# Transposes and down products of an expert chunk placed one chunk behind its gate and up products, in a fixed order of three engines

## The chip, the cores and the metric

The kernel runs on one core of one Trainium2 chip. A core has five engines with queues of their own: TensorE (PE; its weight loads are shown as PEld), VectorE (DVE), ScalarE (ACT), GpSimd (POOL) and SyncE (SP), which here only issues DMA transfers. Sixteen DMA engines move data between HBM and the on-chip memory. The metric is the device time of one execution in microseconds; less is better.

## The reference, cut to what matters

One layer of a hybrid model over 512 tokens of width 1024: a convolution and a gated recurrence (the front part), then a mixture of 16 experts, then a norm. Each expert takes the 64 tokens with the highest affinity to it. The experts are what the change touches:

```python
aff = softmax(einsum('bnd,de->bne', v, router_w))
gate, idx = top_k(swapaxes(aff, 1, 2), 64)      # 64 of 512 tokens for each of 16 experts
xs = v[bidx, idx]
ys = (silu(xs @ wg) * (xs @ wu)) @ wd           # wg, wu: 1024 x 2816; wd: 2816 x 1024, per expert
out = zeros_like(v).at[bidx, idx].add(ys * gate[..., None])
```

All of it is float32. The weights of one expert are 3 x 2816 x 1024 values, 33 blocks of 1 MB (1.0486 million bytes); all 16 experts read 528 blocks once, and no block is used twice.

## The kernel before, in words

**The stream of loads.** The host lays out every weight block as one row of `in_stream`, 128 x 2048 values, in the order that `plan()` gives (L67 to L137). The kernel brings them in by one SP queue, in that order (`issue`, L199), into a ring of 22 buffers (8 + 7 + 7, L187), with two more blocks in another buffer at the start. `take(name, AHEAD)` (L220) issues all loads up to 23 blocks past the one that is asked for; a load into a buffer waits until the block that was there before has been used. For each expert and each chunk j the plan has the gate blocks, the up blocks and the down blocks of chunk j (L129 to L131); for the last two chunks of the last expert the up blocks of both come before the down blocks (L132 to L136).

**The chunks.** The 2816 hidden columns of an expert are cut into five chunks of 512 and one of 256 (`chunks`, L182). For a chunk TensorE multiplies the expert's tokens `xe` with the gate block (`pgu` bank 0) and the up block (bank 1), L1118: two blocks each, one each in the half chunk. ScalarE takes silu of the gate (L1126), VectorE multiplies with the up result (L1129), into `sg`. `turn` (L1036) transposes `sg` on TensorE (`ht`, L1042) and copies it on VectorE (`hT`, L1047). `products_down` (L1052) multiplies `hT` with the down blocks, summed over the chunks in `dn` (L1061).

**The order.** The loop at L1095 writes, for chunk j, first gate and up products of j, then `turn` and `products_down` of chunk j-1 (`pending`, L1133 to L1135). This is the order of the text; from L1121 on the framework's scheduler may reorder the instructions of each engine as they are built, apart from the last two chunks of the last expert, where the order of TensorE is written out (`manual_schedule`, L1103). A written order of all three engines holds over the end of the front part and ends with `tail.close()` at L1091, and again over the last steps from L1164. At run time each engine always works through its own instructions in the order in which they were built.

**Work between experts.** `scatter` (L1019) scales the result of the previous expert into `ys` (L1021), multiplies it with the one-hot rows `ohT` into `sc` (L1029) for four groups of 128 tokens, and adds to the sums `acc` (L1033). It stands behind the last down products of that expert. `combine_weights` (L995) makes `ohT` by transposes (`oht`, L999) at j = 2. `route` (L942) makes the next expert's ranks at j = 3: transposes `rk` on TensorE, comparisons `junk` on VectorE (L959 to L965), one-hot rows `ohr` on VectorE and GpSimd (L954). `gathered` (L971) collects the tokens of the next expert by products with `ohr` (`gx`, L978), two copies (`xg`, L982) and four transposes (`gt`, L985); `dispatch` (L989) makes `xe` in eight steps on VectorE (L992). The buffers for `sc`, `oht`, `rk` and `gt` are one pair of PSUM banks, tag "c".

**The end.** Behind the last down product stand the scaling of it (L1163), its scatter into four row groups (`fin`, L1082 and L1170), the final norm and four stores (L1208).

Of the kernel before, what the change touches and what calls it, by code (L numbers as in the profile page):

```python
# [17 lines left out]
P = 128  # L18
# [48 lines left out]
def plan():  # L67
# [57 lines left out]
    NJ = len(chunks)  # L125
    for e in range(NE):

        ends = e == NE - 1
        for j in range(NJ - 2 * ends):  # L129
            load_up(e, j)  # L130
            load_down(e, j)  # L131
        if ends:  # L132
            load_up(e, NJ - 2)
            load_up(e, NJ - 1)
            load_down(e, NJ - 2)
            load_down(e, NJ - 1)  # L136
# [4 lines left out]
def hybrid_layer(ctx: ExitStack, tc: tile.TileContext, x, vecs, wa, wi, router_w, stream, out):  # L141
# [798 lines left out]
    def route(e, then=None):  # L940
        pr = pc(f"rk{e}")[:, 0, :]
        for i in range(NT):  # L942
            T.transpose(pr[:, i * P:(i + 1) * P], aff[:, i, e:e + 1].to_broadcast([P, P]), ident)  # L943
        if then is not None:
            then()
        cnt = ex.tile([P, NT, 3], F32, tag="cnt", name=f"cnt{e}")
        V.memset(cnt, 0.0)
        junk = ex.tile([P, 512], F32, tag="ys", name=f"junk{e}", bufs=1)
        rank = ex.tile([P, NT], F32, tag="rank", name=f"rank{e}")
        ohr = ex.tile([P, NT, CAP], F32, tag="ohr", name=f"ohr{e}", bufs=1)  # L950

# [5 lines left out]
        for i in range(NT):  # L957
            v = aff[:, i, e:e + 1]
            V.tensor_scalar(junk[:, i * P:N], pr[:, i * P:N], v, None, op0=OP.is_gt, op1=OP.add,  # L959
                            accum_out=cnt[:, i, 0:1])  # L960
            if i:
                V.tensor_scalar(junk[:, 0:i * P], pr[:, 0:i * P], v, None, op0=OP.is_ge, op1=OP.add,
                                accum_out=cnt[:, i, 1:2])
            V.scalar_tensor_tensor(junk[:, i * P:(i + 1) * P], pr[:, i * P:(i + 1) * P], v, earlier,
                                   op0=OP.is_equal, op1=OP.mult, accum_out=cnt[:, i, 2:3])  # L965
            if i:
                ranked(i - 1)
        ranked(NT - 1)
        return ohr, rank

    def gathered(e, ohr):  # L971

        pg = p2(f"gx{e}")
        for i in range(NT):
            for q in range(2):
                for h in range(2):
                    c0 = h * 512 + q * 256
                    T.matmul(pg[64 * h:64 * h + 64, q, 0:256], ohr[:, i, :], x_sb[:, i, c0:c0 + 256],  # L978
                             start=i == 0, stop=i == NT - 1)
        xg = ex.tile([P, 512], F32, tag="ys", name=f"xg{e}", bufs=1)  # L980
        for q, cp in enumerate((V.tensor_copy, S.copy)):
            cp(xg[:, q * 256:(q + 1) * 256], pg[:, q, 0:256])  # L982
        px = pc(f"gt{e}")[:, 0, :]
# [3 lines left out]
        return [px[:, k // 4, k % 4, :] for k in range(KD)]  # L987

    def dispatch(e, px):  # L989
# [3 lines left out]
        return xe, last  # L993
# [25 lines left out]
    def scatter(e, ohT):  # L1019
        ys = ex.tile([P, 512], F32, tag="ys", name=f"ys{e}", bufs=1)  # L1020
        V.tensor_tensor(out=ys, in0=down.pop(e), in1=m5, op=OP.mult)  # L1021
        if e == 0:
# [3 lines left out]
        for i in range(NT):  # L1026
            sc = pc(f"sc{e}_{i}")
            for h in range(2):
                T.matmul(sc[:, h, :], ohT[64 * h:64 * h + 64, i * P:(i + 1) * P], ys[64 * h:64 * h + 64, :],  # L1029
                         start=True, stop=True)  # L1030
            for h in range(2):
                hs_ = slice(h * 512, (h + 1) * 512)
                V.scalar_tensor_tensor(acc3[:, i, hs_], sc[:, h, :], aff[:, i, e:e + 1], prev[:, i, hs_],  # L1033
                                       op0=OP.mult, op1=OP.add)

    def turn(st):  # L1036

        e, j, fw, h, _ = st
# [13 lines left out]
    def products_down(st, halves=(0, 1)):  # L1052
        e, j, fw, _, wdn = st
# [34 lines left out]

    ohr, rank = route(0, rest)
    xe, last_v = dispatch(0, gathered(0, ohr))  # L1090
    tail.close()  # L1091

    later = ExitStack()
    pending = None
    for e in range(NE):  # L1095
        ends = e == NE - 1
        if e:
            xe, _ = dispatch(e, gathered(e, ohr))
        for j, (f0, fw) in enumerate(chunks):
            hw = fw // 2  # L1100
            nl = fw // 256
            if ends and j == NJ - 2:
                later.enter_context(tc.manual_schedule(engines={mybir.EngineType.PE}))  # L1103
                below(0)
            if ends and j >= NJ - 2:
                turn(pending)
            if ends and j == NJ - 2:
                products_down(pending)
            pgu = p2(f"pgu{e}_{j}")
            for gu, nm in enumerate("gu"):  # L1110
                w = [take(f"{nm}{e}_{j}_{s}", AHEAD) for s in range(nl)]
                pp = pgu[:, gu, :]
                kl = KD // nl
                if ends and j == NJ - 1 and gu:
                    below(1, 0)
                for k in range(KD):
                    for h in range(2):
                        last_t = T.matmul(pp[64 * h:64 * h + 64, 0:hw], xe[:, k, :], w[k // kl][:, k % kl, h * hw:(h + 1) * hw],  # L1118
                                 start=k == 0, stop=k == KD - 1)
            if e == 0 and j == 0:  # L1120
                later.enter_context(tc.issue_after(last_t.ins))  # L1121
                later.enter_context(tc.issue_after(last_v.ins))
            pg, pu = pgu[:, 0, :], pgu[:, 1, :]
            wdn = [take(f"d{e}_{j}_{s}", AHEAD) for s in range(nl)]
# [6 lines left out]
            if ends and j == NJ - 1:  # L1131
                break
            if pending is not None and not (ends and j == NJ - 2):  # L1133
                turn(pending)
                products_down(pending)  # L1135
# [13 lines left out]
            if e == 0 and j == 3:  # L1149
                later.close()  # L1150
# [13 lines left out]
    later.enter_context(tc.manual_schedule(engines=ordered))  # L1164
# [57 lines left out]
    later.close()  # L1222
# [37 lines left out]
```

## Time and profile before

| | us |
|---|---|
| median of 3 runs | 1611.38 (1609.38 to 1611.47) |
| the profiled execution, its own time | 1612.04 |
| the profiled execution, span from its first to its last instruction | 1610.2 |
| TensorE busy in the span | 1415.2 (88%) |
| VectorE busy | 549.7 (34%) |
| ScalarE busy | 205.5 (13%) |
| moved by DMA | 601.06 MB, mean 373 GB/s |

The profile is of one execution. A busy share is an average over parts with different limits, and matmuls are pipelined, so a busy TensorE isn't one at its peak. The front part ends, and the first expert's products start, near 304 us; the rest of the span is the experts and some 15 us of ending. An idle stretch of an engine is put down to the instruction that released it. L12 is line 12 of the kernel before.

### The profile page before, as it was taken

How to read it: one execution, taken by the hardware profiler on the slowest of the kernel's cores; microseconds unless marked ns; L12 is line 12 of the kernel's file. 1: busy time of each engine (PE TensorE's matmuls, PEld its weight loads, DVE VectorE, ACT ScalarE, POOL GpSimd, SP SyncE). 2: the span in 40 equal slices, each digit the busy share in tenths (PEclk: the TensorE clock that was granted, in tenths of full speed). 3: DMA queues.
4: the chain of work that ended last, by engine and by line, in shares of the span. 5: the costliest groups of instructions: out<-in, count | busy, mean ns of one | idle time of the engine just before them, and what ended most of it. 6: DMA issues, size and time to landing. Idle time of an engine off the chain costs nothing.

```text
span 1610.2 us, 24198 instructions
## 1 busy us (share of the span) xinstructions
PE 1415.2 (88%) x10345; PEld 847.0 (53%) x10345; DVE 549.7 (34%) x1355; ACT 205.5 (13%) x360; POOL 145.7 (9%) x130
## 2 busy tenths in 40 slices
PE   6996869899988888888989898989898989898997
PEld 5764547676545445454545454545454545454553
DVE  4899995322240403031312121212222222222202
ACT  4676443200000000000000000000000000000001
POOL 3334555000000000000000000000000000000000
PEclk9998889999999999999999999999999999999999
DMA  9532547999999999999999999999999999999971
GB/s 380 188 131 82 206 192 331 363 412 407 422 426 424 425 424 426 424 423 425 425 425 425 424 425 424 425 425 425 425 423 426 424 425 424 425 425 425 424 301 53
DMA packets 86672, 601.06 MB, mean 373 GB/s; under 512 B 12397, under 2 KB 12709, under 8 KB 14117
## 3 DMA queue, kind: packets, MB, share of 16 engines
q1 hardware_dynamic: 86096, 599.10, 89.4%
q8 instruction: 81, 1.33, 0.3%
q10 hardware_dynamic: 469, 0.42, 0.1%
q14 instruction: 26, 0.21, 0.0%
HBM read 597.39 MB, written 2.10 MB: 372 GB/s over the span
## 4 chain that ended last, share of the span: by engine, by line
PE 79%; DVE 15%; issue 3%; ACT 3%; POOL 1%; DMA 0%; DVEq 0%; POOLq 0%; ACTq 0%
PE pgu L1118 39%; PE dn L1061 21%; PE sc L1029 4%; PE gx L978 4%; DVE y L538 3%; DVE sg L1129 1%; DVE hT L1047 1%; PE wocp L453 1%; PE ht L1042 1%; PE oht L999 1%; DVE junk L959 1%; ACT sg L1126 1%; PE pcv L474 1%; PE gt L985 1%; DVE u L593 1%
## 5 line engine op out<-in xcount | busy, mean ns | idle before, releaser
L1061 PE MATMUL dn<-d,hT 128*64 128x512 f32 x1384 | 369.6, 613 | 31.4 <-DVE hT L1047 31.4
L1118 PE MATMUL pgu<-g,xe 128*64 128x256 f32 (+1 forms) x3072 | 354.0, 362 | 0.4 <-DVE xe L992 0.4
L1118 PE MATMUL pgu<-u,xe 128*64 128x256 f32 (+1 forms) x3072 | 337.5, 363 | 0.0
L1118 PEld LDWEIGHTS pgu<-g,xe 128*64 128x64 f32 x3072 | 232.9, 137 | 133.8 <-issue 58.1
L1118 PEld LDWEIGHTS pgu<-u,xe 128*64 128x64 f32 x3072 | 222.3, 137 | 103.2 <-issue 22.9
L1129 DVE TENSOR_TENSOR sg<-sg,pgu 128x256 f32<-128x256 f32 x96 | 38.2, 398 | 594.0 <-ACT sg L1126 594.0
L1061 PEld LDWEIGHTS dn<-d,hT 128*64 128x64 f32 x1384 | 109.3, 139 | 194.6 <-issue 126.9
L1126 ACT ACTIVATE sg<-pgu 128x256 f32<-128x256 f32 x96 | 35.2, 366 | 1197.9 <-PE pgu L1118 1197.9
L954 POOL TENSOR_SCALAR ohr<-iota,rank,rinv 128x64 f32<-128x64 f32 x32 | 18.5, 578 | 1157.6 <-DVE rank L953 1157.6
L1033 DVE SCALAR_TENSOR_TENSOR acc<-sc,aff,acc 128x512 f32<-128x512 f32 x112 | 78.9, 747 | 65.6 <-PE sc L1029 65.6
L1042 PE MATMUL ht<-ident,sg 128*128 128x128 f32 x176 | 40.2, 303 | 57.0 <-DVE sg L1129 55.8
L1029 PE MATMUL sc<-ys,ohT 64*128 64x512 f32 x240 | 67.7, 641 | 16.5 <-DVE acc L1033 16.0
L538 DVE SCALAR_TENSOR_TENSOR y<-glu,dwt,y 128x480 f32<-128x480 f32 (+19 forms) x88 | 81.5, 973 | 0.2
L1042 PEld LDWEIGHTS ht<-ident,sg 128*128 128x128 f32 x176 | 18.3, 140 | 99.5 <-DVE sg L1129 90.3
L978 PE MATMUL gx<-x_sb,ohr 128*64 128x256 f32 x512 | 67.1, 380 | 0.4 <-POOL ohr L954 0.4
L1047 DVE COPY hT<-ht 128x256 f32<-128x256 f32 x95 | 38.0, 400 | 69.7 <-PE ht L1042 69.7
L1001 DVE TENSOR_SCALAR ohT<-oht 128x512 f32<-128x512 f32 (+1 forms) x16 | 11.1, 692 | 128.1 <-PE oht L999 128.1
L978 PEld LDWEIGHTS gx<-x_sb,ohr 128*64 128x64 f32 x512 | 46.6, 137 | 10.6 <-POOL ohr L954 1.1
L959 DVE TENSOR_SCALAR_CACHE_REDUCE junk<-rk,aff 128x512 f32<-128x512 f32 (+1 forms) x64 | 35.0, 546 | 37.2 <-PE rk L943 37.2
L992 DVE TENSOR_SCALAR xe<-gt,a,mods 128x64 f32<-128x64 f32 x128 | 33.8, 337 | 26.6 <-PE gt L985 26.6
L1029 PEld LDWEIGHTS sc<-ys,ohT 64*128 64x128 f32 x240 | 18.1, 184 | 37.5 <-DVE acc L1033 31.3
L577 PE MATMUL pg<-xc,gw 128*128 128x512 f32 x32 | 19.9, 708 | 17.6 <-ACT u L579 16.9
(319 smaller groups left out, 1190.7 us busy)
## 6 DMA issues: line engine op xcount, KB each, us to landing
g<-in_stream SPq DMA_DIRECT2D x176, 1024.0 KB, 19.6
u<-in_stream SPq DMA_DIRECT2D x176, 1024.0 KB, 19.6
d<-in_stream SPq DMA_DIRECT2D x173, 1024.0 KB, 19.6
adam<-in_stream SPq DMA_DIRECT2D x16, 1024.0 KB, 6.8
ada<-in_stream SPq DMA_DIRECT2D x8, 1024.0 KB, 10.9
cv<-in_stream SPq DMA_DIRECT2D x4, 1024.0 KB, 7.7
xs<-in_x SPq DMA_DIRECT2D x4, 512.0 KB, 8.1
lx<-in_stream SPq DMA_DIRECT2D x2, 1024.0 KB, 6.0
```

The source lines that it names most:

```text
L538: V.scalar_tensor_tensor(dst, src, tap(cb, t), dst, op0=OP.mult, op1=OP.add)
L959: V.tensor_scalar(junk[:, i * P:N], pr[:, i * P:N], v, None, op0=OP.is_gt, op1=OP.add, accum_out=cnt[:, i, 0:1])
L978: T.matmul(pg[64 * h:64 * h + 64, q, 0:256], ohr[:, i, :], x_sb[:, i, c0:c0 + 256], start=i == 0, stop=i == NT - 1)
L992: last = V.tensor_scalar(xe[:, k], px[k], a2[:, k:k + 1], SHIFT2[:, k:k + 1], op0=OP.mult, op1=OP.add)
L1029: T.matmul(sc[:, h, :], ohT[64 * h:64 * h + 64, i * P:(i + 1) * P], ys[64 * h:64 * h + 64, :], start=True, stop=True)
L1033: V.scalar_tensor_tensor(acc3[:, i, hs_], sc[:, h, :], aff[:, i, e:e + 1], prev[:, i, hs_], op0=OP.mult, op1=OP.add)
L1042: T.transpose(ptr[:, q2 * P:(q2 + 1) * P], h[:, q2 * P:(q2 + 1) * P], ident)
L1047: V.tensor_copy(hT[:, 0:nq, :], ptr[:, 0:nq * P].rearrange("p (q n) -> p q n", n=P))
L1061: T.matmul(down[e][64 * dh:64 * dh + 64, :], turned[j][:, q2, half * CAP:(half + 1) * CAP], wdn[qq // 2][:, qq % 2, dh * 512:(dh + 1) * 51 ...
L1118: last_t = T.matmul(pp[64 * h:64 * h + 64, 0:hw], xe[:, k, :], w[k // kl][:, k % kl, h * hw:(h + 1) * hw], start=k == 0, stop=k == KD - 1)
L1126: last_s = S.activation(sg[:, 0:hw], pg[:, 0:hw], AF.Silu)
L1129: V.tensor_tensor(out=sg[:, 0:hw], in0=sg[:, 0:hw], in1=pu[:, 0:hw], op=OP.mult)
```

## The change

The plan now gives, for every expert, the gate and up blocks of chunk j and then the down blocks of chunk j-1; the last down blocks of an expert come at its end. The written order of TensorE, VectorE and ScalarE holds from the end of the front part to the end of the kernel (`tail` is closed at the very end; `later` and its ties are gone). In it, chunk j is: gate products of j; silu; transposes and copy of j-1 (`turn`); extra work of this chunk, if any; up products of j; product of silu and up; down products of j-1, whose blocks are taken only there. The scatter of the previous expert is cut into four pieces, two each in chunks 0 and 1. The ranks are cut in two, tiles 0 and 1 in chunk 3, tiles 2 and 3 in chunk 4. At the end of an expert stand the gather of the next one, the transposes of the half chunk, the dispatch of the next expert, the down products of the half chunk, and the scaling into `ys`. The eight steps of `dispatch` go to VectorE and ScalarE by turns.

```diff
-    NJ = len(chunks)
     for e in range(NE):
-        ends = e == NE - 1
-        for j in range(NJ - 2 * ends):
+        for j in range(len(chunks)):
             load_up(e, j)
-            load_down(e, j)
-        if ends:
-            ...
+            if j:
+                load_down(e, j - 1)
+        load_down(e, len(chunks) - 1)
...
         xe = ex.tile([P, KD, CAP], F32, tag="xe", name=f"xe{e}", bufs=XEB)
         for k in range(KD):
-            last = V.tensor_scalar(xe[:, k], px[k], a2[:, k:k + 1], SHIFT2[:, k:k + 1], op0=OP.mult, op1=OP.add)
+            if k % 2:
+                S.activation(xe[:, k], px[k], AF.Identity, bias=SHIFT2[:, k:k + 1], scale=a2[:, k:k + 1])
+            else:
+                V.tensor_scalar(xe[:, k], px[k], a2[:, k:k + 1], SHIFT2[:, k:k + 1], op0=OP.mult, op1=OP.add)
...
     def products_down(st, halves=(0, 1)):
-        e, j, fw, _, wdn = st
+        e, j, fw, _ = st
+        wdn = [take(f"d{e}_{j}_{s}", AHEAD) for s in range(fw // 256)]
...
-    ohr, rank = route(0, rest)
-    xe, last_v = dispatch(0, gathered(0, ohr))
-    tail.close()
-    later = ExitStack()
-    pending = None
+    ohr, rank, ranks = route(0, rest)
+    ranks(0, 1, 2, 3)
+    xe = dispatch(0, gathered(0, ohr))
+    pending = ys = ohT = None
     for e in range(NE):
         ends = e == NE - 1
-        if e:
-            xe, _ = dispatch(e, gathered(e, ohr))
         for j, (f0, fw) in enumerate(chunks):
             ...
             pgu = p2(f"pgu{e}_{j}")
-            for gu, nm in enumerate("gu"):
-                ...
+            products_up(e, j, 0)
             sg = ex.tile([P, 256], F32, tag="sg", name=f"sg{e}_{j}")
-            last_s = S.activation(sg[:, 0:hw], pg[:, 0:hw], AF.Silu)
+            last_s = S.activation(sg[:, 0:hw], pgu[:, 0, 0:hw], AF.Silu)
             ...
-            V.tensor_tensor(out=sg[:, 0:hw], in0=sg[:, 0:hw], in1=pu[:, 0:hw], op=OP.mult)
-            st = (e, j, fw, sg, wdn)
-            if pending is not None and not (ends and j == NJ - 2):
-                turn(pending)
-                products_down(pending)
-                if pending[1] == NJ - 1:
-                    scatter(e - 1, ohT)
+            if j:
+                turn(pending)
+            if j < 2 and e:
+                scatter(e - 1, ohT, ys, 2 * j)
             if j == 2:
-                ohT, gate = combine_weights(e, ohr, rank)
-            pending = st
-            if j == 3 and e + 1 < NE:
-                ohr, rank = route(e + 1)
+                next_ohT, gate = combine_weights(e, ohr, rank)
+            if j == 3 and not ends:
+                ohr, rank, ranks = route(e + 1)
+                ranks(0, 1)
             ...
+            if j == 4 and not ends:
+                ranks(2, 3)
+            if ends and j == NJ - 2:
+                below(0)
+            if ends and j == NJ - 1:
+                below(1, 0)
+            products_up(e, j, 1)
+            V.tensor_tensor(out=sg[:, 0:hw], in0=sg[:, 0:hw], in1=pgu[:, 1, 0:hw], op=OP.mult)
+            st = (e, j, fw, sg)
+            if ends and j == NJ - 1:
+                break
+            if j:
+                products_down(pending)
+            if j < 2 and e:
+                scatter(e - 1, ohT, ys, 2 * j + 1)
+            if j == 2:
+                ohT = next_ohT
+            pending = st
+        if not ends:
+            xg = gathered(e + 1, ohr)
+            turn(st)
+            xe = dispatch(e + 1, xg)
+            products_down(st)
+            ys = weighted(e)
```

## Rows read from the trace of the kernel before

**Rows 1.** The page: busy time by engine; DMA share in 40 slices, in tenths

```profile
PE 1415.2 (88%) x10345; PEld 847.0 (53%) x10345; DVE 549.7 (34%) x1355; ACT 205.5 (13%) x360; POOL 145.7 (9%) x130
DMA  9532547999999999999999999999999999999971
```

**Rows 2.** Waits of TensorE, 400 to 1500 us: us in total, times, longest

```profile
PE ht L1042 <- DVE sg L1129: 52.8, 53, 1.2
PE dn L1061 <- DVE hT L1047: 30.4, 54, 0.7
PE sc L1029 <- DVE acc L1033: 14.9, 13, 1.1
PE rk L943 <- DVE ohT L1001: 10.6, 14, 0.8
PE gt L985 <- DVE xg L982: 3.4, 13, 0.3
```

**Rows 3.** Windows: stretch, length, busy by engine (count), TensorE clock, DMA share, GB/s

```profile
400.00:1500.00 1100.00, 986.80 (x7437) 550.08 (x7435) 257.31 (x815) 34.58 (x94) 16.18 (x28) 0.99 1.01 425
1570.00:1595.00 25.00, 23.56 (x178) 12.00 (x179) 1.89 (x6) 2.15 (x4) 0.00 (x0) 1.00 0.00 1
```

**Rows 4.** Waits of SP's queue, 400 to 1500 us, columns as in rows 2

```profile
SPq L217 <- DMA d<-in_stream: 308.1, 147, 3.3
...
SPq L217 <- PE dn L1061: 54.9, 45, 6.3
```

**Rows 5.** DMA queues, 400 to 1500 us: packets, MB, share of 16 engines

```profile
q1 hardware_dynamic: 63968, 465.87, 100.8%
```

**Rows 6.** Timeline of TensorE: start, length, line, operation, count, [idle before, releaser]

```profile
728.09 3.62 PE L1118 MATMUL pgu<-g,xe 128*64 128x256 f32 x32
...
736.11 0.44 PE L1042 MATMUL ht<-ident,sg 128*128 128x128 f32 x2 [0.94 <-DVE sg L1129]
737.07 3.65 PE L1061 MATMUL dn<-d,hT 128*64 128x512 f32 x16 [0.52 <-DVE hT L1047]
740.55 3.62 PE L1118 MATMUL pgu<-g,xe 128*64 128x256 f32 x32
...
773.36 0.44 PE L985 MATMUL gt<-ident,xg 128*128 128x128 f32 x2 [0.26 <-DVE xg L982]
```

**Rows 7.** One line's instructions (L985): ns min/median/max, first and last start

```profile
L985 PE MATMUL gt<-ident,xg x64: 272/300/332, 302.4 to 1512.2; 128*128 128x128 f32 x64
```

**Rows 8.** Timeline of the end, all engines, columns as in rows 6

```profile
1547.24 0.33 SPq L215 DMA_DIRECT2D d<-in_stream  x1
...
1593.03 1.89 PE L1061 MATMUL dn<-d,x_sb 128*64 128x512 f32 x8
...
1594.96 0.75 DVE L1163 SCALAR_TENSOR_TENSOR hTh<-dn,gate,m 128x512 fp32r<-128x512 f32 x1 [4.17 <-PE dn L1061]
```

**Rows 9.** DMA issues, 1546.6 to 1549 us: count, KB each, median us to landing

```profile
d<-in_stream SPq DMA_DIRECT2D x1, 512.0 KB, 17.1
```

**Rows 10.** Windows of 10 us, columns as in rows 3

```profile
320.00:330.00 10.00, 10.00 (x84) 7.71 (x82) 0.75 (x2) 0.39 (x1) 0.00 (x0) 1.00 0.96 371
390.00:400.00 10.00, 10.00 (x75) 7.70 (x74) 1.29 (x3) 0.38 (x1) 0.00 (x0) 1.00 0.97 364
470.00:480.00 10.00, 7.33 (x43) 3.58 (x41) 5.80 (x29) 0.38 (x1) 1.16 (x2) 0.86 1.02 428
590.00:600.00 10.00, 8.54 (x68) 4.61 (x66) 0.85 (x2) 0.39 (x1) 0.00 (x0) 1.00 1.01 417
800.00:810.00 10.00, 7.32 (x46) 3.29 (x46) 6.49 (x32) 0.38 (x1) 1.16 (x2) 1.00 1.01 425
```

**Rows 11.** The page's groups: count | busy us, mean ns | idle before, releaser

```profile
L1126 ACT ACTIVATE sg<-pgu 128x256 f32<-128x256 f32 x96 | 35.2, 366 | 1197.9 <-PE pgu L1118 1197.9
...
L959 DVE TENSOR_SCALAR_CACHE_REDUCE junk<-rk,aff 128x512 f32<-128x512 f32 (+1 forms) x64 | 35.0, 546 | 37.2 <-PE rk L943 37.2
L992 DVE TENSOR_SCALAR xe<-gt,a,mods 128x64 f32<-128x64 f32 x128 | 33.8, 337 | 26.6 <-PE gt L985 26.6
```

More of the change, by code (lines that the diff above doesn't have):

```diff
@@ L955, in ranked, with ranks @@
                             op0=OP.is_equal, op1=OP.mult)
[L957 to L969, printed above, removed]
+        def ranks(*tiles):
+            for i in tiles:
+                v = aff[:, i, e:e + 1]
+                V.tensor_scalar(junk[:, i * P:N], pr[:, i * P:N], v, None, op0=OP.is_gt, op1=OP.add,
+                                accum_out=cnt[:, i, 0:1])
+                if i:
+                    V.tensor_scalar(junk[:, 0:i * P], pr[:, 0:i * P], v, None, op0=OP.is_ge, op1=OP.add,
+                                    accum_out=cnt[:, i, 1:2])
+                V.scalar_tensor_tensor(junk[:, i * P:(i + 1) * P], pr[:, i * P:(i + 1) * P], v, earlier,
+                                       op0=OP.is_equal, op1=OP.mult, accum_out=cnt[:, i, 2:3])
+                if i:
+                    ranked(i - 1)
+            if i == NT - 1:
+                ranked(i)
+        return ohr, rank, ranks
     def gathered(e, ohr):
@@ L982, in gathered, with dispatch @@
             cp(xg[:, q * 256:(q + 1) * 256], pg[:, q, 0:256])
+        return xg
+    def dispatch(e, xg):
         px = pc(f"gt{e}")[:, 0, :]
@@ L986, in gathered @@
         px = px.rearrange("p (q h s) -> p h q s", h=2, s=CAP)
-        return [px[:, k // 4, k % 4, :] for k in range(KD)]
-    def dispatch(e, px):
+        px = [px[:, k // 4, k % 4, :] for k in range(KD)]
         xe = ex.tile([P, KD, CAP], F32, tag="xe", name=f"xe{e}", bufs=XEB)
         for k in range(KD):
-            last = V.tensor_scalar(xe[:, k], px[k], a2[:, k:k + 1], SHIFT2[:, k:k + 1], op0=OP.mult, op1=OP.add)
-        return xe, last
+            if k % 2:
+                S.activation(xe[:, k], px[k], AF.Identity, bias=SHIFT2[:, k:k + 1], scale=a2[:, k:k + 1])
+            else:
+                V.tensor_scalar(xe[:, k], px[k], a2[:, k:k + 1], SHIFT2[:, k:k + 1], op0=OP.mult, op1=OP.add)
+        return xe
     def combine_weights(e, ohr, rank):
@@ L1017, in hybrid_layer, with weighted, scatter @@
     down = {}
-    def scatter(e, ohT):
+    def weighted(e):
         ys = ex.tile([P, 512], F32, tag="ys", name=f"ys{e}", bufs=1)
         V.tensor_tensor(out=ys, in0=down.pop(e), in1=m5, op=OP.mult)
-        if e == 0:
+        return ys
+    def scatter(e, ohT, ys, i):
+        if not sums:
             sums.append(acc_tile("acc").rearrange("p (i d) -> p i d", i=NT))
@@ L1025, in scatter @@
         prev = x_sb if e == 0 else acc3
[L1026 to L1034, printed above, removed]
+        sc = pc(f"sc{e}_{i}")
+        for h in range(2):
+            T.matmul(sc[:, h, :], ohT[64 * h:64 * h + 64, i * P:(i + 1) * P], ys[64 * h:64 * h + 64, :],
+                     start=True, stop=True)
+        for h in range(2):
+            hs_ = slice(h * 512, (h + 1) * 512)
+            V.scalar_tensor_tensor(acc3[:, i, hs_], sc[:, h, :], aff[:, i, e:e + 1], prev[:, i, hs_],
+                                   op0=OP.mult, op1=OP.add)
     def turn(st):
-        e, j, fw, h, _ = st
+        e, j, fw, h = st
         nq = fw // 2 // P
@@ L1087, in rest, with products_up @@
         table(AF.Silu)
-    ohr, rank = route(0, rest)
-    xe, last_v = dispatch(0, gathered(0, ohr))
-    tail.close()
-    later = ExitStack()
-    pending = None
+    def products_up(e, j, gu):
+        f0, fw = chunks[j]
+        hw, nl = fw // 2, fw // 256
+        w = [take(f"{'gu'[gu]}{e}_{j}_{s}", AHEAD) for s in range(nl)]
+        kl = KD // nl
+        for k in range(KD):
+            for h in range(2):
+                T.matmul(pgu[64 * h:64 * h + 64, gu, 0:hw], xe[:, k, :], w[k // kl][:, k % kl, h * hw:(h + 1) * hw],
+                         start=k == 0, stop=k == KD - 1)
@@ L1163, in hybrid_layer @@
         V.scalar_tensor_tensor(dst, dn, gate, m5, op0=OP.mult, op1=OP.mult)
-    later.enter_context(tc.manual_schedule(engines=ordered))
     low(V, ysl, ys, ysh)
@@ L1221, in hybrid_layer @@
     rows_out(3, 1)
-    later.close()
+    tail.close()
 _OUT = (512, 1024)
```

29 lines of the change are left out of this document (removed).

## The prediction, made before the changed kernel was run

> **What bounds the kernel now.** I read the page's busy shares first. TensorE is busy 1415.2 us of 1610.2, and from the eighth of 40 slices on the 16 DMA engines are in the top tenth in nearly every slice [rows 1]. Two candidates for the bound, then, and an average can't choose between them. So the second view is the waits of TensorE over 400 to 1500 us, a stretch that holds nothing but experts: its idle time is ended by VectorE every time, never by a transfer in any amount [rows 2]. The windows view puts a size on it: 986.80 us busy of 1100, so 113.2 us idle, at DMA share 1.01 [rows 3]. The third view is the queue that issues the loads. SP mostly waits for an earlier load to land (d rows alone 308.1 us in 147 waits) and only 54.9 us in 45 waits for a down product to free a buffer [rows 4]. Loads are thus issued as fast as earlier ones land.
>
> So two streams run side by side at almost the same pace. The stream moves 465.87 MB in 1100 us [rows 5], 423.5 GB/s, so a 1.0486 MB load takes 2.476 us and an expert's 33 loads 81.7 us. TensorE needs from the gather of one expert to that of a later one (1512.2 - 773.4) / 9 = 82.1 us [rows 6, 7], of which 89.7% [rows 3], 73.6 us, are busy. TensorE never waits for a load because it runs behind the stream. How far behind shows at the end: the last load is issued at 1547.24 and takes 17.1 us, so it has landed at 1564.3 [rows 8, 9]; the down product that reads it starts at 1593.03 and ends at 1594.92 [rows 8]. From 1570 to 1595 the DMA engines carry next to nothing while TensorE is 94% busy [rows 3]. **That lag of 29 to 30 us after the last landing is what can be won, and the stream is the floor under it.**
>
> **The change part by part.** I go by the profiled execution: span 1610.2 us, its own time 1612.04, so 1.84 us lie around the span. The median of the three timed runs is 1611.38, 0.66 lower.
>
> *Transposes one chunk later.* A plain chunk now runs gate, up, wait 0.94, transposes 0.44, wait 0.52, down, and repeats after 740.55 - 728.09 = 12.46 us [rows 6]. The transposes wait for silu and product of the very chunk whose up products have just ended; the down products wait for the copy of the transposes. In the new order the transposes of chunk j-1 stand behind gate j (some 3.5 us of TensorE, after down j-2, itself 3.5 us behind the up products that they depend on), and the copy runs under up j (3.5 us). Both waits have a cover of over 3 us for under 1 us of work. Removed: 1.46 us a chunk, leaving 11.0 us, against 6 x 2.476 = 14.9 us of loads. In the stretch that is 52.8 + 30.4 us [rows 2].
>
> *Scatter in four pieces.* The four pairs of products now follow each other and wait up to 1.1 us for the sums of the one before (14.9 us) [rows 2]. Afterwards at least 3.4 us of gate, up or down products stand between two pieces. The sums go into VectorE's queue ahead of the product of silu and up; that product is needed only behind the next gate products. Removed: most of 14.9 us. The 10.6 us of the router's transposes behind the one-hot copy go the same way, since the two now stand in different chunks [rows 2].
>
> *Ranks in two halves.* Two tiles are some five passes of 0.55 us [rows 11], with the small steps 3 to 4 us by estimate, queued in VectorE ahead of the product of chunk 3 and of chunk 4. Those run under up products of 3.5 us; the result is wanted behind down (3.5) and gate (at least 1.8). Cost nothing. The GpSimd one-hots are wanted a chunk later still.
>
> *Gather and dispatch.* The gather now stands alone at the end of an expert, then one transpose pair of the last half chunk, then the four transposes, which wait for two copies. Nothing in the trace shows that exact order; the nearest row is the wait of 0.3 us there now [rows 2], with a copy of VectorE at some 0.5 us in a row with it (the wait of 0.52 behind the copy of the transposes [rows 6]), so 0 to 0.9 us an expert. I take 0.5. The eight xe steps are split over VectorE and ScalarE. ScalarE has no such step in the trace; its nearest row is 366 ns for the silu, VectorE's own step is 337 ns [rows 11], so four in a row take 1.3 to 1.5 us instead of 2.7 for eight. They hide behind the down products of the half chunk (8 matmuls, 1.89 us [rows 8]). Without that cover it is 1.5 us an expert. Either way it comes out of TensorE's spare time, not out of the end.
>
> *Loads in the order of use, down loads taken when used.* SP issues the same loads in another order. Now a down load sits in its buffer one chunk longer than its place in the ring, and every later load queues behind it in SP: the 54.9 us of SP waiting on down products [rows 4]. With several loads in flight most of this costs no bandwidth, since the share stays at 1.01. It cost some at the start: 371 GB/s in 320 to 330 and 364 in 390 to 400 [rows 10] against 424, together 1.25 + 1.4 = 2.7 us. I take that as won; the bounds are 0 and about 6 (twice that, if SP's waits in the steady part cost something too). What is lost before 310 stays, as those buffers only come free when expert 0 begins.
>
> **Sum.** TensorE would need 73.6 us an expert, perhaps 75 with new small waits, against 81.7 of the stream. It gains on the stream 6 to 8 us an expert, has the lag of 29 us used up within four or five experts, and waits for loads from then on. So **of 113 us of removed idle time only the lag counts**. The last landing moves from 1564.3 to 1561.6. Behind it half of the last eight down matmuls, 0.95 us (the last load comes in two halves), 0.1 for the start, and then the ending as it is, from 1594.92 to 1610.2, 15.3 us. Span 1561.6 + 1.05 + 15.3 = 1578.0; with 1.84 around it 1579.8; less the 0.66 by which the profiled execution stands above the median, **1579 us**, 2.0% faster.
>
> **Rivals.**
> *Part of the waits comes back.* Each engine works in its order, so in a new order other instructions can be held up by a late one than now. If 7 of the 8 us an expert return as other waits (the gather's copies, a queue behind the ranks), TensorE needs about 81 us and ends with about 15 us of lag left: 1594. Against it: each cover above is over 1 us longer than what it hides. Chance 0.07. If all comes back, nothing changes: 1611, chance 0.03; this is also the case in which the change doesn't do what it says.
>
> *The stream is not at its limit* and gains 1% when SP never waits for TensorE: 12 us off 1579, 1567. For it: SP waits 45 times for a down product in the steady part [rows 4]. Against it: the lowest 10 us window from 410 to 1550 still has 417 GB/s at share 1.01 [rows 10], though these waits come and go. Chance 0.05. The Trainium skill, "DMA: Bandwidth & Descriptors", section Specifications, states a fabric ceiling of 435 GB/s; by that an estimate of 2.41 us a load would end the stream some 30 us sooner, near 1548 in all. It also states 358 GB/s as a core's limit at the HBM, and there the trace disagrees with its 423.5.
>
> *TensorE waits for loads and its clock falls* (slower). In a plain chunk it would work 11.0 of 14.9 us, 74%. In the present trace two windows at 73% busy have a granted clock of 0.86 (some of the time at the level of 1.2 GHz) and 1.00 [rows 10], so such idling sometimes costs clock. Price: only 10.3% of the stretch is idle [rows 3], at a mean clock of 0.99, so below a mean clock of about 0.89 TensorE alone takes longer than now: from the transposes ahead of expert 0 at 302.4 [rows 7] to 1594.9 are 1292.5 us, 89.7% of them work, 1159; at 0.85 these become 1350, some 58 us more than now, 1669 in all. Against it: once TensorE is behind the stream it no longer waits for loads, and the clock over the experts as they are now is 0.99, so the fall would end itself. A mild form, with the ending alone at the lower clock, adds 2 to 4 us. The Trainium skill, "TensorE: Matmul & The Clock Gate", section "HAM oscillation", states that matmuls separated by waits for DMA can drop to half clock at each wait; the window at 1.00 shows that it need not happen at this busy share. Chance of slower 0.04.
>
> **How the numbers follow.** The forecast (stream as the floor) gets 0.81: 1574 with 6 us won at the loads, 1583 with none, 1587 with the mild clock loss. To leave out no more than 0.2 the range goes from 1571 to 1591; the rivals at 1567, 1594, 1611 and slower lie outside. Faster by over 0.2% (about what a measurement of this kernel can tell from no change): 0.93. Within 0.2%: 0.03. Slower: 0.04.
>
> **What would show it.** In the changed profile: TensorE's waits on the product of silu and up and on the copy are gone, and waits on loads stand in their place from about expert 5 on; the period of an expert there is 81.5 to 82 us, not 74; PE busy about 90% as before, since the floor sets the pace; GB/s in 320 to 400 without dips; the last load lands at 1558 to 1564 and the last down product ends 1 to 2 us after it. Wrong would be: the last down product over 5 us behind the last landing (order leaves waits), a period under 81 us (stream faster), or a granted clock under 0.95 over the experts.

## The result, and the profile after

| | before | after |
|---|---|---|
| median, us | 1611.43 (1609.38 to 1613.87, 4 runs) | 1583.43 (1582.49 to 1585.37, 4 runs) |
| ratio | | 0.9827 [0.981, 0.9844] |
| the profiled execution, its own time | 1612.04 | 1585.37 |
| its span | 1610.2 | 1583.5 |

28.0 us went, 1.7%; the prediction was 1579 with a range of 1571 to 1591. The same kernel measured again beside later experiments gave 1583.32 (0.9825 [0.9811, 0.9839]). The profiled execution of after is the slowest of its four, 1.94 us over their median.

The page of after: busy time by engine, DMA share in 40 slices, and the chain that ended last (followed back from the last instruction, at each step to what released it), by engine. Below it the chain of before.

```profile
PE 1412.9 (89%) x10345; PEld 797.5 (50%) x10345; DVE 542.8 (34%) x1291; ACT 231.4 (15%) x424; POOL 146.9 (9%) x130
DMA  9531547899999999999999999999999999999994
DMA 60%; PE 27%; DVE 10%; ACT 2%; issue 1%; POOL 0%; DVEq 0%; SPq 0%; ACTq 0%; POOLq 0%
```

```profile
PE 79%; DVE 15%; issue 3%; ACT 3%; POOL 1%; DMA 0%; DVEq 0%; POOLq 0%; ACTq 0%
```

Busy time of TensorE hardly moved against [rows 1], and neither did the DMA share. What moved is the chain: it now runs through loads for 60% of the span, where before it ran through TensorE for 79% and through loads for 0%. The busy shares would not have told.

Waits of TensorE in after, 400 to 1500 us (total, times, longest), to be read against [rows 2]:

```profile
PE pgu L1105 <- DMA g<-in_stream: 29.3, 55, 0.7
PE dn L1070 <- DMA d<-in_stream: 25.8, 48, 2.2
PE dn L1070 <- DVE sg L1145: 19.9, 34, 0.6
PE pgu L1105 <- DMA u<-in_stream: 12.2, 40, 0.5
PE gt L988 <- DVE xg L981: 3.8, 14, 0.3
```

The waits of the transposes, of the scatter and of the router's transposes are gone; loads stand in their place. The third row names VectorE's product, on which down products of the chunk before don't depend. A plain chunk shows what it is. Timeline of TensorE in after (start, length, line, operation, count, [idle before, releaser]):

```profile
1049.15 1.95 PE L1105 MATMUL pgu<-g,xe 128*64 128x256 f32 x16 [0.59 <-DMA g<-in_stream]
1051.49 1.95 PE L1105 MATMUL pgu<-g,xe 128*64 128x256 f32 x16 [0.39 <-DMA g<-in_stream]
1053.37 0.44 PE L1050 MATMUL ht<-ident,sg 128*128 128x128 f32 x2
1054.02 1.95 PE L1105 MATMUL pgu<-u,xe 128*64 128x256 f32 x16 [0.21 <-DMA u<-in_stream]
1056.35 1.95 PE L1105 MATMUL pgu<-u,xe 128*64 128x256 f32 x16 [0.38 <-DMA u<-in_stream]
1058.90 1.94 PE L1070 MATMUL dn<-d,hT 128*64 128x512 f32 x8 [0.60 <-DVE sg L1145]
1061.26 1.94 PE L1070 MATMUL dn<-d,hT 128*64 128x512 f32 x8 [0.42 <-DMA d<-in_stream]
1063.77 1.97 PE L1105 MATMUL pgu<-g,xe 128*64 128x128 f32 x32 [0.58 <-DMA g<-in_stream]
```

Six blocks, six starts, 2.44 us apart on average, (1063.77 - 1049.15) / 6: TensorE goes at the pace of the landings. The down products at 1058.90 keep that beat too, so their 0.60 us is read as a load as well, put down to an engine that ended a moment earlier (e4 below bears this out). With these rows 87 us of the 93 idle us (1100 - 1006.98, below) are waits for loads.

Windows of after, columns as in [rows 3]; then one window of before; then SP's waits for down products in 400 to 1500, as in [rows 4]:

```profile
300.00:400.00 100.00, 98.03 (x791) 55.45 (x789) 23.35 (x74) 9.12 (x22) 1.16 (x2) 1.00 0.98 404
310.00:320.00 10.00, 9.89 (x92) 6.29 (x88) 0.84 (x2) 0.38 (x1) 0.00 (x0) 1.00 1.01 388
320.00:330.00 10.00, 10.00 (x84) 5.58 (x82) 1.54 (x3) 0.38 (x1) 0.00 (x0) 1.00 1.02 424
390.00:400.00 10.00, 10.00 (x80) 4.95 (x76) 2.27 (x5) 0.38 (x1) 0.00 (x0) 1.00 1.01 428
540.00:550.00 10.00, 10.00 (x86) 5.75 (x86) 1.53 (x3) 0.38 (x1) 0.00 (x0) 1.00 1.02 420
1040.00:1050.00 10.00, 8.02 (x54) 3.47 (x52) 2.34 (x12) 0.00 (x0) 0.58 (x1) 1.00 1.01 424
400.00:1500.00 1100.00, 1006.98 (x7634) 525.10 (x7632) 256.52 (x776) 57.76 (x152) 16.17 (x28) 1.00 1.01 425
```

```profile
300.00:400.00 100.00, 98.35 (x776) 66.47 (x774) 22.80 (x75) 3.71 (x10) 1.16 (x2) 1.00 0.97 400
```

```profile
SPq L212 <- PE dn L1070: 2.1, 8, 0.3
```

TensorE still works without a pause at 540 to 550 and is down to 8.02 of 10 us at 1040 to 1050. SP's 54.9 us of waiting for down products are gone. The end of after, timeline of all engines, and the landing of its last load (count, KB, median us to landing), as in [rows 8, 9]:

```profile
1548.15 0.33 SPq L210 DMA_DIRECT2D d<-in_stream  x1
```

```profile
d<-in_stream SPq DMA_DIRECT2D x1, 512.0 KB, 17.1
```

```profile
1555.58 1.97 PE L1105 MATMUL pgu<-g,xe 128*64 128x128 f32 x32 [0.62 <-DMA g<-in_stream]
...
1566.42 1.89 PE L1070 MATMUL dn<-d,x_sb 128*64 128x512 f32 x8
...
1568.35 0.75 DVE L1175 SCALAR_TENSOR_TENSOR hTh<-dn,gate,m 128x512 fp32r<-128x512 f32 x1 [4.17 <-PE dn L1070]
```

The last load lands at 1548.15 + 17.1 = 1565.25, the last down product ends at 1568.31. **The last landing has hardly moved (1564.3 before); the lag behind it fell from 30.6 to 3.1 us.** That is 27.5 us. The two profiled spans differ by 26.7, since the last landing of after comes 0.9 us later and its ending is 0.1 us shorter; the medians differ by 28.0.

### The profile page after: what moved, and what is told of

It reads as the page before. It is cut to its first block, busy times and chain, and to the rows that moved or that the text cites. A ratio compares the mean times of both kernels' runs of the same rounds, so it can differ in the third digit from the quotient of the medians.

```text
span 1583.5 us, 24439 instructions
## 1 busy us (share of the span) xinstructions
PE 1412.9 (89%) x10345; PEld 797.5 (50%) x10345; DVE 542.8 (34%) x1291; ACT 231.4 (15%) x424; POOL 146.9 (9%) x130
## 4 chain that ended last, share of the span: by engine, by line
DMA 60%; PE 27%; DVE 10%; ACT 2%; issue 1%; POOL 0%; DVEq 0%; SPq 0%; ACTq 0%; POOLq 0%
DMA d<-in_stream 28%; DMA g<-in_stream 28%; PE pgu L1105 12%; PE dn L1070 5%; DVE y L533 4%; DMA u<-in_stream 4%; PE wocp L448 1%; PE gx L977 1%; PE sc L1037 1%; PE pcv L469 1%; DVE xc L562 1%; DVE u L588 1%; PE plx L448 1%; PE ht L1050 1%; PE pmada L337 0%
## 5 line engine op out<-in xcount | busy, mean ns | idle before, releaser
L1070 PE MATMUL dn<-d,hT 128*64 128x512 f32 x1400 | 331.9, 602 | 46.8 <-DMA d<-in_stream 26.1
L1105 PE MATMUL pgu<-g,xe 128*64 128x256 f32 (+1 forms) x3040 | 326.0, 364 | 31.0 <-DMA g<-in_stream 30.6
L1105 PE MATMUL pgu<-u,xe 128*64 128x256 f32 (+1 forms) x3072 | 331.5, 366 | 14.0 <-DMA u<-in_stream 12.2
L1105 PEld LDWEIGHTS pgu<-g,xe 128*64 128x64 f32 x3040 | 207.3, 137 | 183.9 <-PE dn L1070 48.3
L1105 PEld LDWEIGHTS pgu<-u,xe 128*64 128x64 f32 x3072 | 206.2, 137 | 135.5 <-ACT sg L1119 23.8
L1070 PEld LDWEIGHTS dn<-d,hT 128*64 128x64 f32 x1400 | 94.8, 137 | 229.9 <-issue 128.1
L1145 DVE TENSOR_TENSOR sg<-sg,pgu 128x256 f32<-128x256 f32 x96 | 38.3, 399 | 200.7 <-PE pgu L1105 200.7
L977 PE MATMUL gx<-x_sb,ohr 128*64 128x256 f32 x512 | 58.3, 379 | 0.0
L977 PEld LDWEIGHTS gx<-x_sb,ohr 128*64 128x64 f32 x512 | 37.7, 137 | 24.4 <-issue 8.9
L981 DVE COPY xg<-gx 128x256 f32<-128x256 f32 x16 | 6.8, 424 | 121.2 <-PE gx L977 121.2
L996 DVE TENSOR_SCALAR xe<-gt,a,mods 128x64 f32<-128x64 f32 x64 | 22.0, 344 | 36.5 <-ACT xe L994 23.6
```

The costliest lines, as they stand in the source:

```text
L1070: T.matmul(down[e][64 * dh:64 * dh + 64, :], turned[j][:, q2, half * CAP:(half + 1) * CAP], wdn[qq // 2][:, qq % 2, dh * 512:(dh + 1) * 51 ...
L1105: T.matmul(pgu[64 * h:64 * h + 64, gu, 0:hw], xe[:, k, :], w[k // kl][:, k % kl, h * hw:(h + 1) * hw], start=k == 0, stop=k == KD - 1)
L1145: V.tensor_tensor(out=sg[:, 0:hw], in0=sg[:, 0:hw], in1=pgu[:, 1, 0:hw], op=OP.mult)
```

## The experiments

Theory: the stream of loads is a floor with its end near 1565; TensorE's own pace counts only as far as it closes the lag behind the stream. Rivals: the gain goes with the waits removed; the load order carries it; the floor is something else. "Last landing" and "lag" below are read as above, from the last issue with its time to landing and the end of the last down products, in each one's profiled execution.

| kernel | median, us | ratio to before | last landing | lag |
|---|---|---|---|---|
| before | 1611.4 | | 1564.3 | 30.6 |
| after | 1583.4 | 0.9827 [0.981, 0.9844] | 1565.3 | 3.1 |
| after, measured again | 1583.3 | 0.9825 [0.9811, 0.9839] | 1563.2 | 3.0 |
| e1: old load order | 1589.0 | 0.9859 [0.9835, 0.9882] | 1565.7 | 6.4 |
| e2: shift undone | 1605.9 | 0.9966 [0.9954, 0.9977] | 1563.0 | 25.7 |
| e3: load order alone, engines as the scheduler places them | 1592.5 | 0.9884 [0.9866, 0.9901] | 1564.2 | 12.3 |
| e4: after, no down loads | 1453.8 | 0.9022 [0.8999, 0.9046] | | |
| e5: shift undone, no down loads | 1607.4 | 0.9968 [0.9956, 0.9979] | | |
| e6: 7.1 us more TensorE an expert | 1590.6 | 0.9864 [0.9846, 0.9882] | 1567.0 | 7.6 |
| e7: 14.2 us more | 1683.3 | 1.0443 [1.0419, 1.0468] | 1615.3 | 49.9 |
| e8: three buffers less | 1591.8 | 0.9875 [0.9859, 0.9891] | 1571.5 | 2.4 |
| e9: ending moved | 1581.8 | 0.9812 [0.9798, 0.9826] | 1562.6 | 1.2 |
| e10: old load order but in the last expert | 1584.3 | 0.9829 [0.9815, 0.9843] | 1565.3 | 4.3 |

**TensorE's own pace, without a third of the stream (e4, e5).** One down block is loaded once, and all down products read it; the other down loads are left out, and the ring has one buffer less for it.

```diff
-        wdn = [take(f"d{e}_{j}_{s}", AHEAD) for s in range(fw // 256)]
+        wdn = [dfix, dfix]
```

> The changed kernel without its 176 loads of down blocks: all down products read one block that is loaded once, so the result is another one; the ring has one buffer less to hold it. The stream falls to 22 loads an expert, 54.7 us at 2.488 us a load. Theory (the changed kernel waits for the stream, and TensorE alone would be faster): the expert takes TensorE's own time, 70.8 us as between experts 1 and 3 of the changed kernel, so 305 + 69 + 15 x 70.8 + 17 = 1453 us, 1440 to 1465, with hardly a wait of TensorE for a load. Rival (TensorE needs its 82 us an expert whatever the loads do): over 1560.

> The fixed order with the transposes and down products right behind the up products of the same chunk (the shift undone), and without the 176 loads of down blocks: all down products read one block, so the result is another one. It shows TensorE's own pace in that order. Theory: 80.4 us an expert, 1590 to 1610 us in all, and the same kernel with its loads is no faster than that and no faster than the stream lets it (1583). Rival (without the stream both orders are alike): as the changed kernel without these loads, about 1453.

The transposes of the gather show the pace: one line's instructions, ns min/median/max, first and last start. After, then e4, then e5:

```profile
L988 PE MATMUL gt<-ident,xg x64: 272/300/333, 304.1 to 1488.4; 128*128 128x128 f32 x64
```

```profile
L991 PE MATMUL gt<-ident,xg x64: 272/300/329, 301.3 to 1358.8; 128*128 128x128 f32 x64
```

```profile
L997 PE MATMUL gt<-ident,xg x64: 272/300/332, 303.3 to 1508.1; 128*128 128x128 f32 x64
```

Fifteen experts in each: 79.0, 70.5 and 80.3 us an expert. The new order needs 70.5 us when the stream lets it; in after it takes 79.0, and from the gather at 1077.00 to the one at 1487.78, five experts later, 82.2. A window of e4:

```profile
400.00:1400.00 1000.00, 993.03 (x7808) 542.33 (x7806) 263.88 (x794) 58.66 (x154) 16.28 (x28) 1.00 0.83 315
```

TensorE stands idle for 7 us of 1000 there, and the row "dn L1070 <- DVE sg L1145" of after (19.9 us) has no counterpart among its waits, although TensorE reaches the down products sooner: those 19.9 us were waits for down blocks.

Without the shift TensorE needs 80.3 us whether a third of the loads is there or not: 1607.4 without, 1605.9 with (next, where the same count also gives 80.3). So unshifted, TensorE is the bound; shifted, the stream is. Free of the stream the shift is worth 153.6 us; with it, 17 (e2 against e1, both in the old load order).

**The shift undone, the rest kept (e2).**

```diff
-            if j:
-                turn(pending)
+            if ends and j == NJ - 1:
+                turn(pending)
...
-            if j:
-                products_down(pending)
+            if not (ends and j == NJ - 2):
+                turn(st)
+                products_down(st)
```

> The changed kernel with the fixed order kept, but the transposes and down products of a chunk right behind its own up products, with the load order of before. Scatter in four pieces, split ranks and split dispatch stay. Theory (only the lag counts, and TensorE's own pace decides how much of it is closed): TensorE pays the two waits of 0.94 and 0.52 us again in each of six chunks and some 1 us at the gather, about 80.4 us an expert instead of 71, against 82.1 of the stream. It closes 1.7 us an expert, some 20 to 28 us of the 29 in all: 1585 to 1603 us. Rival (the shift is the whole gain): 1608 to 1612. Rival (the shift does nothing, the other parts carry the gain): 1582 to 1584, with no lag left behind the last landing.

Timeline of TensorE in e2, a plain chunk:

```profile
752.53 0.44 PE L1056 MATMUL ht<-ident,sg 128*128 128x128 f32 x2 [0.59 <-DVE sg L1151]
753.49 3.65 PE L1076 MATMUL dn<-d,hT 128*64 128x512 f32 x16 [0.52 <-DVE hT L1061]
```

1605.9, 3 us over the theory's range, and neither rival: both waits are back, the first shorter (0.59), and only 5.6 us of the gain are left. The pace was right (80.4 expected); the lag to be closed was not. It isn't the 29 us that before ended with, but what the stream is ahead after the first experts, and the first expert itself was slower here than in before's built order: TensorE worked 88.70 us of 300 to 400, against 98.35 in before (its row stands with the result). Window of e2:

```profile
300.00:400.00 100.00, 88.70 (x689) 46.79 (x687) 19.29 (x60) 6.93 (x18) 1.16 (x2) 1.00 0.98 403
```

**The old load order under the new engine order (e1), and in all but the last expert (e10).** In e1 `plan()` is that of before. In e10 experts 0 to 14 load the down blocks of chunk j behind the up blocks of j, and expert 15 loads as in after.

> The changed kernel with one part undone: the loads come in the order of before (down blocks of chunk j right behind its gate and up blocks), the order of the engines stays the new one. Theory (the stream of loads is the floor, and the engine order alone lets TensorE close the lag of 29 us): the stream carries the same bytes, so 1583 us, 1580 to 1587; the last landing stays near 1565. Rival (the order of the loads carries a part of the gain, because a down block that waits a chunk in the ring holds up the loads behind it): 1589 us or more, with SP waiting for down products again as in before (54.9 us in 400 to 1500).

> The loads in the order of before for experts 0 to 14 and in the new order for the last expert alone. In the profile with the old order throughout TensorE waited 2.01 us for the last full gate block (1546.15 instead of 1540.97 in after), since the two down blocks of chunk 3 were loaded ahead of it, 2 x 2.49 = 5 us; from there it works without a pause. Theory (the order of the loads matters in the last expert alone): 1583 us, as after. Rival (it matters in every expert): 1588 to 1590, as with the old order throughout.

Timeline of TensorE in e1, then the same block in e10:

```profile
1540.54 3.60 PE L1076 MATMUL dn<-d,hT 128*64 128x512 f32 x16
1546.15 1.95 PE L1111 MATMUL pgu<-g,xe 128*64 128x256 f32 x16 [2.01 <-DMA g<-in_stream]
```

```profile
1544.30 3.62 PE L1107 MATMUL pgu<-g,xe 128*64 128x256 f32 x32
```

e1 lost 5.5 us, as the rival said, but not by its mechanism: SP waited for down products 9.9 us in 400 to 1500, not 54.9, and the last landing stayed. Its lag is 3.3 us longer than in after, and it arose in the last expert, where two down blocks stand ahead of the last full gate block. With the new order there alone, 1584.3 is 0.9 us over after beside it, and their runs overlap. So **in experts 0 to 14 the order of the loads is worth at most about 1 us**.

**The load order without the written order (e3).** The order of the engines is left to the scheduler as in before, the down blocks are taken in the down products and no longer in the loop ahead of the activation, and `plan()` is that of after.

```diff
-            wdn = [take(f"d{e}_{j}_{s}", AHEAD) for s in range(nl)]
+        wdn = [take(f"d{e}_{j}_{s}", AHEAD) for s in range(fw // 256)]
```

> The kernel of before with the load order of after alone, down blocks taken when used; the engines are ordered by the scheduler as before. Built so, a plain chunk runs gate, up, transposes of this chunk, down products of the chunk before: the wait of 0.94 us for the product of silu and up stays, the 0.52 us behind the copy is covered. Theory (only the lag counts): the waits behind the copy were 30.4 us over 13.4 experts, 2.3 us an expert; without them TensorE needs about 79.8 us against 82.1 of the stream and closes nearly all of the lag: 1584 to 1593 us. Rival (the gain goes with all of the waits removed, in proportion): a quarter of the gain, 1604 us. Rival (the loads' order gains nothing by itself): 1610 to 1613.

A wait of TensorE in 400 to 1500 us, then one row of its timeline:

```profile
PE ht L1036 <- DVE sg L1123: 59.1, 53, 1.7
```

```profile
1549.61 6.10 PE L1056 MATMUL dn<-d,hT 128*64 128x512 f32 x16 [8.76 <-DMA d<-in_stream]
```

1592.5, in the theory's range: 19 of 28 us come with one of the two waits gone and the larger one kept, far from "in proportion" (1604). This isn't the worth of the load order by itself: the scheduler built another order of TensorE with it, the down products a chunk behind, and e10 shows that under a fixed engine order the loads' order gives at most about 1 us ahead of the last expert. 8.76 us of its lag of 12.3 stand in the last expert, where its written order asks for the down blocks of chunk 3 ahead of the gate blocks that are loaded first.

**TensorE made slower (e6, e7).** Extra matmuls with the gate blocks, overwritten by the real ones: the diff is that of e6, and e7 has `range(6)`.

```diff
+        if not gu:
+            for k in range(3):
+                for h in range(2):
+                    T.matmul(pgu[64 * h:64 * h + 64, 0, 0:hw], xe[:, k, :], w[k // kl][:, k % kl, h * hw:(h + 1) * hw],
+                             start=True, stop=True)
```

> The changed kernel with more work for TensorE: in each chunk the gate products of the first 3 of 8 blocks of rows are made once more ahead of the real ones, 1.3 us in a chunk of 512 and 0.65 in the half chunk, 7.1 us an expert; the result is the same. Theory (the stream is the floor, TensorE has 82.1 - 70.8 = 11 us to spare in an expert): 77.9 us an expert is still under the stream, it closes the lag in 7 experts instead of 4, and the time stays: 1582 to 1587. Rival (TensorE sets the time): 16 x 7.1 = 114 us more, 1697.

> As the kernel with 3 blocks of gate products made twice, but 6 of 8: 14.2 us more of TensorE in an expert. Theory: 85.0 us an expert, over the stream's 82.1, so TensorE is the bound again: 305 + 83 + 15 x 85 + 17 = 1680 us, 1665 to 1695, and the lag behind the last landing is back at over 25 us. Rival (there is more to spare than 11 us an expert): under 1620. Rival (TensorE sets the time throughout): 1583 + 16 x 14.2 = 1810.

SP's waits in e7, 400 to 1500 us, and its window:

```profile
SPq L212 <- PE pgu L1110: 573.9, 220, 5.1
```

```profile
400.00:1500.00 1100.00, 1094.64 (x9045) 626.00 (x9042) 241.24 (x725) 54.36 (x143) 15.01 (x26) 1.00 1.00 408
```

114 us more work for TensorE (16 x 7.1) cost 7.3 us; twice that cost 100. The knee lies between, as the theory has it: over the stream's pace TensorE sets the time again, the lag is 50 us, and the stream is held back to 408 GB/s. The theory missed 7 us of e6. Its last landing is 1.7 us later and its lag is 7.6 us. The end of e6, timeline of TensorE:

```profile
1530.96 3.60 PE L1070 MATMUL dn<-d,hT 128*64 128x512 f32 x16
1534.39 1.46 PE L1106 MATMUL pgu<-g,xe 128*64 128x256 f32 x12
```

```profile
1572.73 1.89 PE L1070 MATMUL dn<-d,x_sb 128*64 128x512 f32 x8
```

TensorE waits for no load any more in the last expert and works without a pause from 1525.98 to the last down product. The reading is this: every expert falls behind the stream at its gather and scatter and makes it up in its plain chunks, 3.9 us each in after (14.9 - 11.0) and 2.6 in e6; in the last expert, which also has the transposes and sums of the ending to do, e6 has not made it up when the loads end. No run tests this by itself.

**What sets the floor (e8).**

```diff
-RC = 7
+RC = 4
```

> The changed kernel with 19 buffers in the ring instead of 22. Theory (the floor is the stream that starts once the first expert frees its buffers; what was loaded before is the number of buffers): three loads of 2.488 us fewer lie ahead of the first expert, so the last landing and the end come 7.5 us later: 1591, 1588 to 1594. Rival (the loads in flight alone set the pace of the stream, and the buffers behind them cost nothing): 1582 to 1585. Rival (with 19 buffers the gather and scatter of an expert starve the stream): over 1600, with GB/s dips in the steady part.

The last load of e8, its issue and its time to landing:

```profile
1553.56 0.33 SPq L210 DMA_DIRECT2D d<-in_stream  x1
```

```profile
d<-in_stream SPq DMA_DIRECT2D x1, 512.0 KB, 17.9
```

8.4 us more, in the theory's range and 0.9 over the three loads that it counted; the last landing is at 1571.5, 8.2 us behind that of after measured again, whose first gate products began within 0.1 us of those of e8. The stream carries 424 GB/s from 400 to 1500, so the third rival didn't come either. The number of buffers sets what is loaded before the first expert frees one; the rest of the stream runs at its own pace from there.

**The rest of the lag (e9).** In the last expert the matmuls that put the sums under the results of the second row group move ahead by a chunk, and those of the third stand behind the products of the last chunk, the second half of them behind those of the first two row groups.

```diff
-            if j:
+            if ends and j == NJ - 2:
+                pgu = p2(f"pgu{e}_{NJ - 1}")
+                products_down(pending, (0,))
+                below(1, 0)
+                products_down(pending, (1,))
+                below(1, 1)
+            elif j:
                 products_down(pending)
...
-    below(1, 1)
...
-    below(2, 0)
...
-    below(2, 1)
+    below(2, 0)
...
+    below(2, 1)
```

> The changed kernel as it is, on the same chip as the two that follow, as their measure: 1583 us, 1581 to 1586.

> The changed kernel with 5 of the 6 matmuls that put the old sums under the last results moved: two each beside the down products of chunk 3 of the last expert, where TensorE waits for loads, two behind the last down products, where it waits for VectorE. In the profile of after TensorE works without a pause from 1555.58 to 1568.31, 12.7 us, while only 9.7 us of loads are still to land. Theory (behind the floor only this last piece of lag, 3 us, is left): the last down product ends 1 to 1.5 us behind the last landing instead of 3.0, and the first scatter follows sooner: 1.5 to 2.5 us less than after, 1581 to 1582. Rival (the ending is bound by its own chain on ScalarE and VectorE): no difference to after.

The end of e9, timeline of TensorE:

```profile
1561.88 1.89 PE L1070 MATMUL dn<-d,x_sb 128*64 128x512 f32 x8
```

The last down product ends 1.2 us behind the last landing instead of 3.0, and the median is 1.55 us under after beside it, as the theory has it. Both intervals against before overlap, so as a faster kernel it isn't shown; that the lag is 1.8 us shorter in the profile is.

## Why the prediction was right, and where it was off

*The bound and the lag.* Right. The lag was used up, the waits became waits for loads, and the last landing of all kernels with the full stream and 22 buffers stayed between 1562.6 and 1567.0 us, e7 apart, while their times differ by 30 us. The 82.1 us that it gave TensorE count from the first transposes of one gather to the last of another; from first to first it is 81.9 (773.36 to 1510.62, nine experts), 0.2 us over the stream's 81.7. That changes nothing in the argument. The lag was used up after four experts; four or five were forecast.

*The waits that go.* Right: both waits of a chunk, the scatter's and the router's are gone. TensorE's pace was put at 73.6 to 75 us and is 70.5 (e4): busy time counts the end of a group of matmuls that the next group already overlaps. In the rows of e6 above a group of 3.60 us starts only 3.43 us ahead of the next.

*The sum.* 1578.0 was the span, 1583.5 came. Two terms were mis-sized. The last landing was put at 1561.6 and came at 1565.25, 3.65 us later. The dips at 320 and 390 us are gone (424 and 428 GB/s against 371 and 364 in [rows 10]), but the first gate products began at 305.41 in this execution against 303.66 in before, and counted from there the last landing is 0.8 us sooner, not 2.7. A part of the dips has only moved: at 310 to 320 it is 388 GB/s against 416 in before, and over 300 to 400 as a whole 404 against 400, which is 0.9 us at 424 GB/s. In the execution measured again they began at 303.04, and the last landing is at 1563.2, by the same count 0.5 us sooner than in before. So the term of 2.7 us for the dips was too large. What lies behind the landing was put at 1.05 us and is 3.06. The other step that failed is that TensorE has caught up with the stream at the very end. It hasn't: from 1555.58 to 1568.31 it has 12.7 us of work for 9.7 us of loads, of which the matmuls that put the sums under the results are a part (e9). 3.65 + 2.0 make the difference, less 0.1 in the ending; the profiled execution's 1.94 over its median, where 0.66 was allowed, takes 1.3 back. Both misses showed in the signs that it had named: a last landing at 1558 to 1564, and a last down product 1 to 2 us behind it.

*The step on the loads.* Its reason was wrong. It said that a down block now waits a chunk longer in the ring. That is the order of the text. In the built order, [rows 6], the down products follow the transposes of the same chunk, so plan and use agreed. The new load order is needed because the engine order is shifted, and then in the last expert, ahead of which it is worth at most about 1 us (e10). The 54.9 us for which SP waited for down products went with the order of the engines: e1, with the old load order, has 9.9.

*Ranks, dispatch.* No wait of TensorE for any of them but 3.8 us at the gather, about the 3.4 of before. The estimate of 0.5 us an expert more was too high.

*The rivals.* None set the time. The clock in after: with 20% of the window idle, in waits of 0.2 to 0.6 us, the granted clock at 1040 to 1050 is 1.00, the level of 2.4 GHz. The Trainium skill, "TensorE: Matmul & The Clock Gate", section "HAM oscillation", describes matmuls between waits for DMA that drop to half clock; the trace shows none of it at waits this short. In after itself the clock fell once between 400 and 1500, to 0.83 in 740 to 750, where TensorE had waited 1.99 us for a down block. In two other orders it fell more often. In e1 and e10 the loads of an expert come in another order, and TensorE waits for gate blocks in fewer and longer pieces: 30 of the 63 waits of e1 for them last 1.95 us or more. The granted clock over 400 to 1500 is 0.98 in both, so a part of that time is at the level of 1.2 GHz, against 1.00 in after. In e3 the sixteen products behind the wait of 8.76 us took 6.10 us instead of 3.65. Waits of TensorE and window of e1, 400 to 1500; window of e3 behind that wait:

```profile
PE pgu L1111 <- DMA g<-in_stream: 86.6, 63, 3.4
```

```profile
400.00:1500.00 1100.00, 1001.75 (x7612) 542.47 (x7610) 255.35 (x773) 57.75 (x152) 16.17 (x28) 0.98 1.01 425
```

```profile
1550.00:1560.00 10.00, 10.00 (x58) 4.85 (x56) 0.00 (x0) 0.00 (x0) 0.00 (x0) 0.77 0.61 256
```

In e10 this and the old load order together cost 0.9 us, which fits the time that TensorE has to spare in an expert. The stream: 425 GB/s with SP's waits for TensorE gone, as with them. The 435 GB/s that the Trainium skill, "DMA: Bandwidth & Descriptors", section Specifications, names as the fabric's ceiling is reached in no 1100 us stretch of any run here.

## What to carry to other kernels

Where an engine and a stream of loads run at nearly the same pace, measure how far the last use lies behind the last landing: that, and not the engine's idle time, is the most that a better order can give: here the lag was 30.6 us, the gain 28.0 and the idle time 113. Once the stream is the floor, what counts is the number of buffers that are full before their first use (8.4 us for three of them here) and the work that is left when the last blocks land. Take the order of an engine from the trace or the built program, not from the text, when a scheduler may move instructions.

## What the runs showed of the hardware

The busy share of the DMA engines doesn't tell whether they are the bound: 1.01 in before, where TensorE was, 1.01 in after, where they are, and 1.00 in e7, where TensorE held them back to 408 GB/s.

In e2 SP waited 238.7 us for gate and up products and 138.8 us for down products in 400 to 1500, and the stream still carried 425 GB/s. Rows of e2, SP's waits, then its window:

```profile
SPq L218 <- PE pgu L1111: 238.7, 148, 6.9
...
SPq L218 <- PE dn L1076: 138.8, 80, 3.1
```

```profile
400.00:1500.00 1100.00, 986.34 (x7596) 517.22 (x7592) 256.55 (x772) 55.81 (x147) 16.17 (x28) 1.00 1.01 425
```

With 19.3 to 19.5 us from issue to landing (the page of e2) and 2.48 us a load, some eight loads are in flight by estimate, and issues that came up to 6.9 us late cost nothing here: the last landing is at 1563.0, no later than in after.
